# Reordering the beginning of a hybrid decoder layer: memory products first, then the products on a once-normed h

## The chip, the core and the metric

The kernel runs on one core of a Trainium2 chip. The metric is device microseconds of one execution. A profile of one execution shows, per engine, every instruction with its start and duration: TensorE (PE, with its weight loads as PEld), VectorE (DVE), ScalarE (ACT), GpSimd (POOL), and the queues that issue transfers (SP, and the transfer-issuing parts of ACT and POOL).

## The reference, cut to what matters

One layer, x of 512 x 2048 in f32, memory of 256 x 2048:

```
h = rmsnorm(x, norm_g)                      # one factor per token, times a gain per channel
(a_q, a_ckv, i_q, i_k, i_w, ..., mix_gate) = split(h @ w_in)
m_k, m_v = split(rmsnorm(mem, mem_norm_g) @ w_mem_kv)
ckv = rmsnorm(a_ckv, kv_norm_g);  a_k, a_v = split(ckv @ w_kv_up)
... three attention branches, gated, projected up, merged, then
x = x + merged @ w_o
```

All products are kept at nearly f32 accuracy: each factor is split into a high part (rounded to the chip's fast f32 form) and a low part (the rest), and three products high x high, high x low, low x high are summed.

## The kernel before

The activations stand transposed: h is 16 slices of 128 channels by 512 tokens, with high parts in `hth` and low parts in `htl`. Weights come from memory in units of 128 x 1024, three buffers deep (`wraw`); each half (512 columns) is split by `split`: ACT casts the high part `wh`, DVE subtracts to get the low part `wl`. A global counter of such halves is the program's clock: `next_hb()` advances it by one step, `step(i)` splits the half that is used four steps later (`LA = 4`) and then runs whatever `plan(i, f)` has put at this step. So all engines get their instructions in an order written out by hand, and each engine executes its own list strictly in order. Background generators (`pump`) advance by one `yield` a step and put their instructions between.

The program begins with these stages:

1. **g1** (16 steps): a group of 336 columns of w_in (the latent `a_ckv`, the index key and index weights) times h. Per step `x_split` makes a high and a low part of x times the gain, not yet of h; the token factor is applied to the result afterwards (L457, L459). ACT squares x (`x_sq`, L379) and POOL adds the squares into `accx` (L380). At the end `g_rms` turns the sum into the token factors `rx` and spreads them over a tile `rb`. A step has 12 products of 336 columns.
2. **mem** (32 steps): mem times w_mem_kv, 6 products of 512 columns a step, four PSUM banks. `m_split` splits two slices of mem every fourth step. Beside it `g_lat` norms the latent, and `g_comb` makes the final h: per round k (8 of them, over slices k and k+8) DVE norms x again with `rb` (L544), ACT casts high parts (L537), DVE and POOL make low parts (L534), and POOL forms four sums and differences of quarter blocks (L559 to L562), whose high parts ACT casts into `hx` (L572) and whose low parts POOL subtracts (L553). These sums feed a seven-product (Strassen-like) scheme that the rest of the kernel uses.
3. **kv** (3 units, n = 0, 1, 2): the latent times w_kv_up, 12 groups of 6 products of 512 columns; `kv_group` squares, sums (DVE `ss` L467), takes a power on POOL (`r`, L304), scales (`t`, L674) and transposes on PE (L678). Before n = 2 the program text waits until `g_comb` has put out all its instructions.
4. **pairs**: the large stage with seven products per weight pair, from the first `p<-hth,wh` on. Its first weights A11 and S1 are loaded by SP when the mem buffers are given back; POOL adds a further block onto S1 by a transfer that accumulates (L217) and sums S1 and A11 (`wS`, L211).

Of the kernel before, what the change touches and what calls it, by code (L numbers as in the profile page):

```python
# [110 lines left out]
def hybrid_layer(ctx: ExitStack, tc: tile.TileContext, xT, memT, memR, w_g1, w_un, w_up, params, consts, rel1, onehot, out):  # L111
# [286 lines left out]

    for c in range(8):
        if c:  # L400
            plan(2 * c - 8, lambda c=c: x_dma(c))
    for k in range(KT):
        plan(k - 4 - (k == 0), lambda k=k: x_split(k))
        plan(k - 3, lambda k=k: x_sq(k))
    i_mem = POS["mem", 0]
    for c in range(8):
        i = i_mem + 4 * c
# [12 lines left out]
    t = wp.tile([128, 1024], F32, tag="raw", bufs=3, name=nm("wraw"))  # L420
    for k in range(2):
        sync.dma_start(xf(k), xT[k].rearrange("p (a b) -> p a b", a=2))
        sync.dma_start(t[:, k * WG:k * WG + WG], w_g1[0, :, k * WG:k * WG + WG])
    tiles_["g1", 0] = t
    for i in range(-8, 0):
        step(i)
        if i == -6:
            sync.dma_start(cc, consts)

    def g_rms():  # L430

        sm = yield from take("sm")
        for i in range(4):
            mmf(sm[:, i:i + 1], accx[:, i * 128:i * 128 + 128], ones1)
        yield from lag("r0")
        done["rx"] = r = rsq(sm[:, :4], 4, 1.0 / D, EPS)
        give("sm")
        yield from lag("r1")
        b = yield from take("sm")
        bcast(b, r, 4)  # L440
        yield from lag("r2")
        act.copy(rb, b)
        give("sm")
        done["rb"] = True
# [81 lines left out]
    def g_comb():  # L526

        while "rb" not in done:
            yield

        nxt, f = {}, None

        def low(k, j, e):
            e.tensor_tensor(out=htl[:, k + 8 * j, :], in0=nxt[k][:, j, :], in1=hth[:, k + 8 * j, :].bitcast(F32), op=ALU.subtract)  # L534

        def high(k, j):
            act.copy(hth[:, k + 8 * j, :], nxt[k][:, j, :])  # L537

        def norm(k, j):
            if k < 8:  # L540
                if j == 0:
                    nxt[k] = cb.tile([128, 2, T], F32, tag="xr", bufs=2, name=nm("xr"))
                v = nxt[k][:, j, :].rearrange("p (a b) -> p a b", a=2)
                dve.scalar_tensor_tensor(v, xf(k + 8 * j), prm(P_NG + k + 8 * j), rb.rearrange("p (a b) -> p a b", a=2),  # L544
                                         op0=ALU.mult, op1=ALU.mult)

        norm(0, 0)
        norm(0, 1)
        yield
        for k in range(9):  # L550
            if k:
                low(k - 1, 0, dve)
                pool_e.tensor_tensor(out=hxt[k - 1][:, 3:6, :], in0=f, in1=hxt[k - 1][:, 0:3, :].bitcast(F32), op=ALU.subtract)  # L553
            if k == 8:
                break
            yield from lag("cb0")
            f = cb.tile([128, 3, 256], F32, tag="tf", bufs=1, name=nm("tf"))
            b11, b12, b21, b22 = (nxt[k][:, j, c:c + 256] for j in range(2) for c in (0, 256))
            pool_e.tensor_tensor(out=f[:, 1, :], in0=b12, in1=b22, op=ALU.subtract)  # L559
            pool_e.tensor_tensor(out=b12, in0=b11, in1=b12, op=ALU.subtract)  # L560
            pool_e.tensor_tensor(out=f[:, 0, :], in0=b22, in1=b12, op=ALU.add)
            pool_e.tensor_tensor(out=f[:, 2, :], in0=b21, in1=f[:, 0, :], op=ALU.subtract)  # L562
            high(k, 1)
            norm(k + 1, 0)
            yield from lag("cb1")
            low(k, 1, pool_e)
            yield from lag("cb2")
            high(k, 0)
            norm(k + 1, 1)
            yield from lag("cb3")  # L570
# [893 lines left out]
```

## Time and profile before

| | |
|---|---|
| three runs | 1613.4, 1618.41 (median), 1621.61 us |
| profiled execution | 1609.5 us, of which span 1607.7 us |
| PE busy in the span | 1506.1 us (94%) |
| DVE, ACT, POOL busy | 1281.3, 794.1, 665.8 us |
| granted TensorE clock, mean | 0.983 |

In the views a releaser ("<-") is what ended an engine's wait. Durations of consecutive instructions on one engine overlap a little, since the next starts before the last has quite ended. [...]

### The profile page before, as it was taken

To read this page: it belongs to the slowest core of one execution; us is meant where nothing else is said; L and a number is where in the kernel's file an instruction comes from. 1 tells how busy PE (TensorE), PEld (TensorE's weight loads), DVE (VectorE), ACT (ScalarE), POOL (GpSimd) and SP (SyncE) were. 2 spreads that over 40 slices of the span, in tenths; PEclk is the share of its full clock that TensorE was granted. 3 is DMA by queue.
4 is the path that set the end of the run, shared out by engine and by line. 5 is a ranking of instruction groups with operands and counts; after the bars stand their busy time and mean duration, and the time that the engine had idled before them with its cause. 6 is when DMAs were issued, how large, how long until landed. Compare 5 with 4: busy or idle time off the path is not lost.

```text
span 1607.7 us, 29512 instructions
## 1 busy us (share of the span) xinstructions
PE 1506.1 (94%) x11066; PEld 1418.6 (88%) x11066; DVE 1281.3 (80%) x1965; ACT 794.1 (49%) x1681; POOL 665.8 (41%) x548
## 2 busy tenths in 40 slices
PE   8778988989989999999999999999989999989999
PEld 6657988889889999999999899898989888869999
DVE  8997678999998678788777787887767567997786
ACT  7545466654545454555454545555545322434442
POOL 5675342333334344333333343333324013775453
PEclk9988999999999999999999999999999999989999
DMA  6337669445446655646555555455456655555774
GB/s 213 131 127 182 170 187 241 118 126 154 122 138 177 189 160 173 182 126 182 177 126 179 147 138 161 119 157 132 141 145 201 219 191 184 177 152 170 205 207 135
DMA packets 98792, 263.75 MB, mean 164 GB/s; under 512 B 10356, under 2 KB 24052, under 8 KB 98650
## 3 DMA queue, kind: packets, MB, share of 16 engines
q1 hardware_dynamic: 81050, 201.97, 35.9%
q0 software_dynamic: 15264, 55.58, 19.0%
q10 hardware_dynamic: 2336, 4.33, 1.1%
q8 instruction: 87, 1.43, 0.3%
q14 instruction: 55, 0.45, 0.1%
HBM read 237.12 MB, written 29.04 MB: 166 GB/s over the span
## 4 chain that ended last, share of the span: by engine, by line
PE 58%; DVE 23%; issue 7%; ACT 4%; DMA 3%; POOL 3%; SPq 0%; ACTq 0%; DVEq 0%; POOLq 0%
PE p L292 18%; PE p L293 18%; PE p L294 18%; DVE wl L276 12%; PE p L297 2%; ACT wh L274 2%; DVE Wk L850 1%; DMA wA<-in_w_un 1%; PE p L955 1%; DVE t L785 1%; DVE m L888 1%; POOL wS L211 1%; DVE Wk L889 1%; POOL r L304 1%; DVE htl L1266 1%
## 5 line engine op out<-in xcount | busy, mean ns | idle before, releaser
L292 PE MATMUL p<-hth,wh 128*128 128x256 f32 (+1 forms) x1792 | 529.7, 296 | 9.9 <-ACT hth L1264 5.5
L294 PE MATMUL p<-hth,wl 128*128 128x256 f32 (+1 forms) x1792 | 519.0, 290 | 1.5 <-DVE wl L276 1.4
L293 PE MATMUL p<-htl,wh 128*128 128x256 f32 (+1 forms) x1792 | 518.0, 289 | 2.3 <-DVE htl L1266 2.3
L276 DVE TENSOR_TENSOR wl<-wS,wh 128x512 fp32r<-128x512 f32 x318 | 318.3, 1013 | 98.7 <-ACT wh L274 94.6
L292 PE MATMUL p<-hx,wh 128*128 128x256 f32 x1272 | 370.4, 291 | 4.8 <-ACT kb L1084 3.3
L294 PE MATMUL p<-hx,wl 128*128 128x256 f32 x1272 | 363.1, 285 | 1.7 <-DVE wl L276 1.6
L276 DVE TENSOR_TENSOR wl<-wraw,wh 128x512 fp32r<-128x512 f32 (+2 forms) x346 | 302.5, 887 | 77.4 <-ACT wh L274 76.6
L292 PEld LDWEIGHTS p<-hth,wh 128*128 128x128 f32 x1792 | 343.8, 192 | 21.1 <-ACT hth L1264 5.7
L293 PE MATMUL p<-hx,wh 128*128 128x256 f32 x1272 | 361.9, 285 | 0.0
L293 PEld LDWEIGHTS p<-htl,wh 128*128 128x128 f32 x1792 | 343.7, 192 | 8.7 <-DVE htl L1266 2.6
L294 PEld LDWEIGHTS p<-hth,wl 128*128 128x128 f32 x1792 | 343.6, 192 | 6.8 <-DVE wl L276 3.0
L211 POOL TENSOR_TENSOR wS<-wS,wA 128x512 f32<-128x512 f32 x106 | 152.8, 1463 | 439.5 <-DMA wA<-in_w_un 247.4
L292 PEld LDWEIGHTS p<-hx,wh 128*128 128x128 f32 x1272 | 246.0, 193 | 10.4 <-ACT kb L1084 3.4
L274 ACT CAST wh<-wraw 128x512 fp32r<-128x512 f32 (+2 forms) x346 | 202.3, 590 | 105.4 <-PE p L293 66.6
L294 PEld LDWEIGHTS p<-hx,wl 128*128 128x128 f32 x1272 | 245.6, 193 | 3.4 <-DVE wl L276 3.4
L293 PEld LDWEIGHTS p<-hx,wh 128*128 128x128 f32 x1272 | 246.0, 193 | 1.1
L274 ACT CAST wh<-wS 128x512 fp32r<-128x512 f32 x318 | 193.8, 618 | 88.1 <-POOL wS L211 41.7
L276 DVE TENSOR_TENSOR wl<-wA,wh 128x512 fp32r<-128x512 f32 x212 | 171.9, 811 | 36.9 <-ACT wh L274 35.2
L211 POOL TENSOR_TENSOR wS<-wraw,wS 128x512 f32<-128x512 f32 x106 | 168.6, 1674 | 8.9 <-DVE wl L276 8.9
L274 ACT CAST wh<-wA 128x512 fp32r<-128x512 f32 x212 | 124.2, 618 | 72.1 <-DMA wA<-in_w_un 39.1
L304 POOL TENSOR_TENSOR r<-rv,cc 128x4 f32<-128x4 f32 (+2 forms) x30 | 41.6, 1388 | 136.9 <-DVE rv L303 136.9
L800 POOL TENSOR_TENSOR t<-u,u 128x256 f32<-128x256 f32 x35 | 37.4, 1068 | 124.2 <-DVE u L799 84.8
(225 smaller groups left out, 2108.4 us busy)
## 6 DMA issues: line engine op xcount, KB each, us to landing
wraw<-in_w_un SPq DMA_DIRECT2D x133, 512.0 KB, 5.4
wS<-in_w_un SPq DMA_DIRECT2D x53, 512.0 KB, 5.8
wA<-in_w_un SPq DMA_DIRECT2D x53, 512.0 KB, 3.7
wS<-in_w_un POOLq DMA_DIRECT2D x53, 512.0 KB, 7.7
wA<-in_w_un POOLq DMA_DIRECT2D x53, 512.0 KB, 5.2
th_d<-t SPq DMA_DIRECT2D x48, 256.0 KB, 4.4
t<-th_d SPq DMA_DIRECT2D x48, 256.0 KB, 3.0
wraw<-in_w_up SPq DMA_DIRECT2D x32, 384.0 KB, 3.7
```

The costliest lines, as they stand in the source:

```text
L211: pool_e.tensor_tensor(out=tiles_[key][:, s], in0=tiles_[a][:, s], in1=tiles_[b][:, s], op=op)
L274: act.copy(h[:, :w], s)
L276: e.tensor_tensor(out=l[:, :w], in0=s, in1=h[:, :w].bitcast(F32), op=ALU.subtract)
L292: pe.matmul(o, ah, bh, start=first, stop=False, skip_group_check=True)
L293: pe.matmul(o, ah, bl, start=False, stop=False, skip_group_check=True)
L294: pe.matmul(o, al, bh, start=False, stop=last, skip_group_check=True)
L297: pe.matmul(o, a, b, start=first, stop=last)
L304: pool_e.tensor_tensor(out=r[:, :n], in0=v[:, :n], in1=cc[:, C_NH:C_NH + n], op=ALU.pow)
L785: dve.tensor_tensor(out=t, in0=p, in1=ev[u], op=ALU.add)
L800: pool_e.tensor_tensor(out=o[1][:, 256:], in0=ev["u3"], in1=ev["u5"], op=ALU.subtract)
L850: dve.scalar_tensor_tensor(s, rl[:, :w], iwt[:, ti, h:h + 1], s, op0=ALU.mult, op1=ALU.add)
L888: dve.max(out=m8, in_=s)
```

## The change

The stages come in the order mem (11 of 16 slices, 22 steps), g1 (16 steps), mem (the last 10 steps), kv. While the first mem steps run, x is loaded by ACT's transfer queue, squared by ACT, and summed by DVE, one slice a step. Then the token factors are made (`rms_sum`, `rms_pow`, `rms_rows`, each planned at a step), and x is normed in place: `x_norm` writes h over x and casts the high part, `x_low` makes the low part. g1 thus uses the final h, in the order 0, 8, 1, 9, ..., and its result needs no factor. `g_comb` keeps only the quarter sums, all on DVE, with the high half-slices on ACT; POOL has no elementwise work left in the beginning except the powers. g1's weights are packed on the host in the new order of slices.

```diff
-    singles("g1", ...)
-    singles("mem", un[:16])
+    singles("mem", un[:K1])          # K1 = 11
+    singles("g1", [w_g1[k] for k in range(8)])
+    singles("mem2", un[K1:16])
...
-            sync.dma_start(xf(k), xT[k]...)                      # x_dma, two slices at a time
+            act.dma_start(xf(k), xT[k]...)
...
-        act.activation(hi, xf(k), AF.Copy, scale=prm(P_NG + k))  # x_split
-        dve.scalar_tensor_tensor(lo, xf(k), prm(P_NG + k), hi...)
-            pool_e.tensor_tensor(out=accx, in0=accx, in1=sq, op=ALU.add)
+        dve.tensor_tensor(out=accx, in0=accx, in1=sqs.pop(k), op=ALU.add)   # x_sum
+    def x_norm(k):
+        dve.scalar_tensor_tensor(xf(k), xf(k), prm(P_NG + k), rb..., op0=ALU.mult, op1=ALU.mult)
+        act.copy(hth[:, k, :]..., xf(k))
+    def x_low(k):
+        dve.tensor_tensor(out=lo, in0=xf(k), in1=hi.bitcast(F32), op=ALU.subtract)
...
+    KO = [k + 8 * j for k in range(8) for j in range(2)]
+    for k in range(KT):
+        plan(k - 6, x_dma(k)); plan(k - 2, x_sq(k)); plan(k - 1, x_sum(k))   # k > 0 for the sum
+    plan(KT, rms_sum); plan(KT + 1, rms_pow); plan(KT + 2, rms_rows)
+    for n, k in enumerate(KO):
+        plan(i_g1 - 2 + n, x_norm(k)); plan(i_g1 - 1 + n, x_low(k))
...
+    mem(range(K1))
     g1 = ...
-    act.activation(zt[:, i, :], g1[i][:, :WG], AF.Copy, scale=done["rx"][:, i:i + 1])
+    act.copy(zt[:, i, :], g1[i][:, :WG])
...
-    def g_comb():   # per k: norm twice, high twice, low on DVE and POOL, 5 POOL operations, lags cb0 to cb3
+    def g_comb():
+        def low(k):
+            dve.tensor_tensor(out=htl[:, k, 256:], in0=xf(k)[:, 1, :], in1=hth[:, k, 256:]..., op=ALU.subtract)
+            hx_new(k, F32R)
+            act.copy(hxt[k][:, 0:3, :], f)
+        def low3(k):
+            dve.tensor_tensor(out=hxt[k][:, 3:6, :], in0=f, in1=hxt[k][:, 0:3, :]..., op=ALU.subtract)
+        for k in range(8):
+            dve.tensor_tensor(out=f[:, 1, :], in0=b12, in1=b22, op=ALU.subtract)
+            dve.tensor_tensor(out=b12, in0=b11, in1=b12, op=ALU.subtract)
+            act.copy(hth[:, k, 256:], b12)
+            dve.tensor_tensor(out=f[:, 0, :], in0=b22, in1=b12, op=ALU.add)
+            dve.tensor_tensor(out=f[:, 2, :], in0=b21, in1=f[:, 0, :], op=ALU.subtract)
+            low(k)
+            yield from lag("cb0")
+            low3(k)
+            yield from lag("cb1")
-    mb = [...]; for k in range(KT): ...          # all 32 mem steps
+    mem(range(K1, KT))
...
+    while "lat" not in done:
+        pump()
```

The lags of `g_lat` (l0 to l3) go from 5, 3, 3, 4 to 2 each, and the fourth mem bank is `sm` instead of `o`. The tile of x for slices k and k+8 (`hx`) is the one that later holds round k's high and low parts of the quarter sums.

The first place is DVE's list during g1 (names: `hx` is x, `htl` low parts of h, `wl` low parts of weights, `t_2` the sum of squares). Before, one g1 step and the next:

```order
L372 SCALAR_TENSOR_TENSOR htl<-hx_149,pc,hth 128x512
L276 TENSOR_TENSOR wl_233<-wraw_162,wh_232 128x336
L372 SCALAR_TENSOR_TENSOR htl<-hx_164,pc,hth 128x512
L276 TENSOR_TENSOR wl_258<-wraw_162,wh_257 128x336
L372 SCALAR_TENSOR_TENSOR htl<-hx_166,pc,hth 128x512
```

In the changed kernel, at the same place in g1:

```order
L394 SCALAR_TENSOR_TENSOR hx_133<-hx_133,pc,rb_114 128x512
L278 TENSOR_TENSOR wl_560<-wraw_483,wh_559 128x336
L399 TENSOR_TENSOR htl<-hx_133,hth 128x512
L394 SCALAR_TENSOR_TENSOR hx_133<-hx_133,pc,rb_114 128x512
L278 TENSOR_TENSOR wl_579<-wraw_511,wh_578 128x336
L399 TENSOR_TENSOR htl<-hx_133,hth 128x512
```

A step has three instructions on DVE instead of two: the norm, which is now here and no longer in the mem stage, a weight split, and the low part, which needs ACT's cast of the normed slice in between.

The second place is one round of `g_comb`. Before, DVE's list in the mem stage (`xr` the normed x, `ml` low parts of mem); its quarter sums are on POOL:

```order
L276 TENSOR_TENSOR wl_859<-wraw_791,wh_858 128x512
L544 SCALAR_TENSOR_TENSOR xr_845<-hx_147,pc,rb_114 128x512
L276 TENSOR_TENSOR wl_875<-wraw_791,wh_874 128x512
L396 SCALAR_TENSOR_TENSOR ml_879<-mr_793,pc,mh_878 128x256 x2
L534 TENSOR_TENSOR htl<-xr_774,hth 128x512
L276 TENSOR_TENSOR wl_895<-wraw_827,wh_894 128x512
L544 SCALAR_TENSOR_TENSOR xr_912<-hx_149,pc,rb_114 128x512
L276 TENSOR_TENSOR wl_915<-wraw_827,wh_914 128x512
```

In the changed kernel, DVE's list for one round (`tf` the quarter sums):

```order
L562 TENSOR_TENSOR tf_954<-hx_141 128x256
L563 TENSOR_TENSOR hx_141<-hx_141 128x256
L565 TENSOR_TENSOR tf_954<-hx_141 128x256
L566 TENSOR_TENSOR tf_954<-hx_141,tf_954 128x256
L552 TENSOR_TENSOR htl<-hx_141,hth 128x256
L278 TENSOR_TENSOR wl_964<-wraw_889,wh_963 128x512
L557 TENSOR_TENSOR hx_961<-tf_954,hx_961 128x768
L278 TENSOR_TENSOR wl_977<-wraw_889,wh_976 128x512
```

and ACT's list for the same round of the changed kernel and the beginning of the next:

```order
L564 CAST hth<-hx_141 128x256
L554 CAST hx_961<-tf_954 128x768
L276 CAST wh_963<-wraw_889 128x512
L276 CAST wh_976<-wraw_889 128x512
L564 CAST hth<-hx_149 128x256
```

DVE now does five short operations and one long one a round where it did two norms and a low part, and POOL none where it did six. ACT's 768-column cast stands ahead of the weight casts, and it writes over the tile of x that DVE's L552 reads.

The third place is POOL's list at the end of `g_comb`. Before:

```order
L562 TENSOR_TENSOR tf_1095<-xr_1044,tf_1095 128x256
L534 TENSOR_TENSOR htl<-xr_1044,hth 128x512
L553 TENSOR_TENSOR hx_1153<-tf_1095,hx_1153 128x768
L217 DMA wS_227_1124<-in_w_un 128x1024
L211 TENSOR_TENSOR wS_245_1188<-wS_227_1124,wA_228_1126 128x512
L304 TENSOR_TENSOR r_1205<-rv_1204,cc 128x2
```

In the changed kernel, from the first power of the program:

```order
L306 TENSOR_TENSOR r_464<-rv_463,cc 128x4
L306 TENSOR_TENSOR r_912<-rv_911,cc 128x4
L218 DMA wS_216_1083<-in_w_un 128x1024
L212 TENSOR_TENSOR wS_237_1162<-wS_216_1083,wA_217_1085 128x512
L306 TENSOR_TENSOR r_1180<-rv_1179,cc 128x2
```

The transfer onto S1 no longer stands behind 48 elementwise operations of `g_comb`; the powers of the kv groups still stand behind the sum `wS`.

## Rows read from the trace of the kernel before

**Rows 1.** stretches: window, busy (xcount) of PE, PEld, DVE, ACT, POOL, clock, DMA, GB/s

```profile
0.00:45.50 45.50, 38.64 (x211) 32.64 (x212) 37.57 (x43) 29.96 (x58) 23.77 (x20) 1.00 0.66 219
45.50:129.00 83.50, 65.63 (x237) 48.85 (x236) 82.33 (x85) 46.44 (x86) 63.03 (x50) 0.86 0.39 135
129.00:149.60 20.60, 13.64 (x54) 10.47 (x53) 10.54 (x26) 7.33 (x19) 9.75 (x11) 0.83 0.66 154
149.60:1607.70 1458.10, 1388.23 (x10571) 1326.63 (x10569) 1150.87 (x1813) 710.34 (x1522) 569.25 (x468) 0.99 0.57 164
```

**Rows 2.** DVE, timeline in g1: start us, us, line, operation

```profile
28.14 0.74 DVE L372 SCALAR_TENSOR_TENSOR htl<-hx,pc,hth 128x512 fp32r<-128x512 f32 x1
28.80 0.49 DVE L276 TENSOR_TENSOR wl<-wraw,wh 128x336 fp32r<-128x336 f32 x1
29.22 1.78 DVE L372 SCALAR_TENSOR_TENSOR htl<-hx,pc,hth 128x512 fp32r<-128x512 f32 x1
```

**Rows 3.** POOL, timeline of the same stretch

```profile
28.93 3.23 POOL L380 TENSOR_TENSOR t<-t,sq 128x512 f32<-128x512 f32 x2 [2.16 <-ACT sq L379]
```

**Rows 4.** DVE, timeline of one round in the mem stage

```profile
107.03 2.88 DVE L276 TENSOR_TENSOR wl<-wraw,wh 128x512 fp32r<-128x512 f32 x2
...
110.50 0.68 DVE L276 TENSOR_TENSOR wl<-wraw,wh 128x512 fp32r<-128x512 f32 x1
...
116.86 2.89 DVE L276 TENSOR_TENSOR wl<-wraw,wh 128x512 fp32r<-128x512 f32 x2
```

**Rows 5.** PE, timeline in the mem stage

```profile
61.03 0.39 PE L294 MATMUL mb<-wh,ml 128*128 128x512 f32 x1
61.26 0.39 PE L292 MATMUL mb<-wh,mh 128*128 128x512 f32 x1
...
79.73 0.79 PE L293 MATMUL mb<-wl,mh 128*128 128x512 f32 x1 [2.25 <-DVE wl L276]
```

**Rows 6.** POOL and DVE, timeline of the tail of kv

```profile
130.82 0.40 DVE L467 TENSOR_REDUCE ss<-sq 128x2 f32<-128x256 f32 x1
...
136.55 1.25 POOL L211 TENSOR_TENSOR wS<-wS,wA 128x512 f32<-128x512 f32 x1 [7.00 <-DMA wS<-in_w_un]
137.77 1.38 POOL L304 TENSOR_TENSOR r<-rv,cc 128x2 f32<-128x2 f32 x2
138.51 0.42 DVE L674 TENSOR_TENSOR t<-pk,r 128x256 f32<-128x256 f32 x1 [6.16 <-POOL r L304]
```

**Rows 7.** PE, timeline, first product of the pairs

```profile
149.67 0.36 PE L292 MATMUL p<-hth,wh 128*128 128x256 f32 x1
```

**Rows 8.** ACT and PE, timeline of the first products

```profile
5.09 0.45 ACT L274 CAST wh<-wraw 128x336 fp32r<-128x336 f32 x1
...
5.59 0.42 PE L292 MATMUL g<-wh,hth 128*128 128x336 f32 x1
```

**Rows 9.** windows at the start, columns as in Rows 1

```profile
5.00:10.00 5.00, 4.30 (x21) 2.92 (x20) 2.94 (x5) 3.38 (x8) 0.13 (x1) 1.00 1.02 351
10.00:20.00 10.00, 7.43 (x45) 6.59 (x44) 9.57 (x7) 10.00 (x21) 9.32 (x7) 1.00 0.57 206
```

**Rows 10.** a group of DVE over the whole span

```profile
L1284 DVE TENSOR_TENSOR f<-m,f 128x256 f32<-128x256 f32 x1 | 0.4, 418 | 0.0
```

**Rows 11.** groups of 0 to 150 us: count, busy us, mean ns

```profile
L274 ACT CAST wh<-wraw 128x512 fp32r<-128x512 f32 x38 | 23.0, 617 | 7.5 <-DMA wraw<-in_w_un 4.1 <-PE g L294 3.4
...
L572 ACT CAST hx<-tf 128x768 fp32r<-128x768 f32 x8 | 6.6, 830 | 0.9 <-POOL tf L562 0.7
```

**Rows 12.** ACT and its transfer queue, timeline

```profile
247.16 0.63 ACTq L722 DMA_DIRECT2D ra_d<-rel_d  x1
247.68 0.61 ACT L833 CAST stk<-t 64x512 fp32r<-64x512 f32 x1
```

**Rows 13.** transfer issues of the page: KB, median us to landing

```profile
wS<-in_w_un SPq DMA_DIRECT2D x53, 512.0 KB, 5.8
...
wS<-in_w_un POOLq DMA_DIRECT2D x53, 512.0 KB, 7.7
```

More of the change, by code (lines that the diff above doesn't have):

```diff
@@ L91 @@
          ("S3", "T3", False), ("S4", "B22", False), ("A22", "T4", True)]
+K1 = 11
 LA = 4
@@ L397, in m_split @@
         MS[c] = (h, l)
-    for c in range(8):
[L400 to L407, printed above, removed]
+    KO = [k + 8 * j for k in range(8) for j in range(2)]
+    for k in range(KT):
+        plan(k - 6, lambda k=k: x_dma(k))
+        plan(k - 2, lambda k=k: x_sq(k))
+        if k:
+            plan(k - 1, lambda k=k: x_sum(k))
+    plan(KT, rms_sum)
+    plan(KT + 1, rms_pow)
+    plan(KT + 2, rms_rows)
+    i_g1 = POS["g1", 0]
+    for n, k in enumerate(KO):
+        plan(i_g1 - 2 + n, lambda k=k: x_norm(k))
+        plan(i_g1 - 1 + n, lambda k=k: x_low(k))
+    for c in range(8):
+        i = POS["mem", 2 * c] if 2 * c < K1 else POS["mem2", 2 * c - K1]
         plan(i - 8, lambda c=c: m_dma(c))
@@ L419, in hybrid_layer, with mem @@
     sync.dma_start(pc, params)
[L420 to L424, printed above, removed]
+    for f in at.pop(-8):
+        f()
+    raw(("mem", 0), un[0])()
     for i in range(-8, 0):
         step(i)
[L427 to L444, printed above, removed]
+    plan(2, lambda: sync.dma_start(cc, consts))
+    mb = [psum(t, "mb") for t in ("qk", "qk", "pt", "sm")]
+    def mem(ks):
+        for k in ks:
+            mh, ml = MS[k // 2]
+            for half in range(2):
+                wh, wl = next_hb()
+                for i in range(2):
+                    s = slice(i * 128, i * 128 + 128)
+                    mm3(mb[2 * half + i], mh[:, k % 2, s], ml[:, k % 2, s], wh, wl, k == 0, k == KT - 1)
+                pump()
+    mem(range(K1))
     g1 = [psum(t, "g1") for t in ("o", "a", "b", "c")]
-    for k in range(KT):
+    for n, k in enumerate(KO):
         wh, wl = next_hb()
@@ L456, in hybrid_layer @@
         if i % 2 == 0:
-            act.activation(zt[:, i, :], g1[i][:, :WG], AF.Copy, scale=done["rx"][:, i:i + 1])
+            act.copy(zt[:, i, :], g1[i][:, :WG])
         else:
-            dve.tensor_scalar(out=zt[:, i, :], in0=g1[i][:, :WG], scalar1=done["rx"][:, i:i + 1], scalar2=None, op0=ALU.mult)
+            dve.tensor_copy(out=zt[:, i, :], in_=g1[i][:, :WG])
     dve.tensor_scalar(out=hb, in0=prm(P_GB, 48), scalar1=0.5, scalar2=None, op0=ALU.mult)
@@ L493, in g_lat @@
             dve.scalar_tensor_tensor(ckl[:, j, :], b[j], prm(P_KVG + j), ckh[:, j, :].bitcast(F32), op0=ALU.mult, op1=ALU.subtract)
+        done["lat"] = True
     def g_ik():
@@ L526, in g_comb @@
     def g_comb():
[L528 to L570, printed above, removed]
+        f = None
@@ L571, in g_comb @@
+        def low(k):
+            dve.tensor_tensor(out=htl[:, k, 256:], in0=xf(k)[:, 1, :], in1=hth[:, k, 256:].bitcast(F32), op=ALU.subtract)
             hx_new(k, F32R)
             act.copy(hxt[k][:, 0:3, :], f)
+        def low3(k):
+            dve.tensor_tensor(out=hxt[k][:, 3:6, :], in0=f, in1=hxt[k][:, 0:3, :].bitcast(F32), op=ALU.subtract)
+        for k in range(8):
+            f = cb.tile([128, 3, 256], F32, tag="tf", bufs=2, name=nm("tf"))
+            b11, b12, b21, b22 = (xf(k + 8 * j)[:, c, :] for j in range(2) for c in range(2))
+            dve.tensor_tensor(out=f[:, 1, :], in0=b12, in1=b22, op=ALU.subtract)
[7 more added lines that the diff above has]
+            yield from lag("cb1")
@@ L576, in hybrid_layer @@
     pump.back(g_comb())
-    mb = [psum(t, "mb") for t in ("qk", "qk", "pt", "o")]
-    for k in range(KT):
-        if k % 2 == 0:
-            mh, ml = MS.pop(k // 2)
-        for half in range(2):
-            wh, wl = next_hb()
-            for i in range(2):
-                s = slice(i * 128, i * 128 + 128)
-                mm3(mb[2 * half + i], mh[:, k % 2, s], ml[:, k % 2, s], wh, wl, k == 0, k == KT - 1)
-            pump()
+    mem(range(K1, KT))
     def scaled(r, n):
@@ L599, in hybrid_layer @@
     give("pt")
+    give("sm")
     mp_s.close()
```

41 lines of the change are left out of this document (24 added, 17 removed).

## The prediction

> **What bounds the kernel now.** I read the page's 40 slices first: PE is busy above 80% everywhere except in the first tenth. So I cut the span there [rows 1]. After 149.6 us PE is busy 1388 of 1458 us; the change touches only what is before, 150 us in which PE is busy 118. In the long second stretch (45.5 to 129 us, the mem stage) the busy engine is DVE, 82.3 of 83.5 us, at a mean clock of 0.86.
>
> Second, DVE's timeline, to see why it is full. The same instruction takes 0.74 us at 28.14 and 1.78 at 29.22 [rows 2], and the second lies inside a POOL addition that runs from 28.93 on [rows 3]: while POOL works on tiles, DVE's two-input operations take about twice as long. In the mem stage a round of four steps takes 9.83 us, from 107.03 to 116.86 [rows 4], with weight splits of 0.68 when POOL is idle and 1.44 (2.88 for two) when it isn't. PE's products follow each other at 0.23 us at full clock [rows 5], so four steps of six are 5.5 us. DVE sets the round; PE waits, 2.25 us at one place [rows 5].
>
> Third, the tail of kv. DVE has its sum ready at 130.82, but the power on POOL comes only at 137.77, since POOL stands at the sum `wS`, which waits 7.00 us for a transfer; DVE waits 6.16 us for the power and PE for DVE [rows 6]. The first pair product starts at 149.67 [rows 7]. That is the moment I compute for the changed kernel; what follows is the same work, bound by PE.
>
> **The change, stage by stage.** Durations are those with POOL idle, since POOL now has only powers. Back to back an instruction costs 0.07 less than its duration (28.14 + 0.74 against 28.80 [rows 2]); from one engine to the next I add 0.05 (5.09 + 0.45 to 5.59 [rows 8]).
>
> Stage 1, 22 mem steps. The first product now needs a weight unit of 0.52 MB instead of 0.17, and x shares the engines; 0.35 to 0.85 MB more at 351 GB/s [rows 9] is 1.0 to 2.4 us, and a second weight cast and two casts of mem stand before it on ACT, about 1.2: 5.6 + 1.7 + 1.2 = 8.4 us. PE needs 22 x 6 x 0.23 = 30.4. While x comes (14 steps), two steps move 1.18 MB (a weight unit, two slices of x, half a tile of mem), 3.36 us at 351 GB/s against 2.74 of PE: 7 x 0.6 = 4.3 more. End: 43 us. DVE lies below it: 22 splits of 0.61 and 4 of 0.42, 15 sums of 0.61, 12 splits of mem of 0.41 (a two-input operation on 256 columns [rows 10]) are 29 us; ACT has 26 casts of weights, 16 squares and 12 small casts, about 31 us by 0.62 for 512 columns [rows 11]. ACT's issuing of x costs it nothing: an issue of 0.63 us ran beside casts [rows 12]. If the transfers run faster, the floor is PE's, 39; bounds 39 to 47 while the rate stays above 300 GB/s.
>
> Stage 2, g1. A step is a chain: norm 0.74 (as L372 with POOL idle [rows 2]), ACT's cast 0.62, low part 0.61, three handovers: 2.07 us; the weight split of 0.42 lies beside the cast. PE's 12 products of 336 columns are 12 x 0.15 = 1.83, so the chain sets the pace. The first norm can start about three mem steps before stage 1 ends, its low part is there 2.5 us before, 15 more chains are 31.0, and the last step's products take 1.9: 30.5 us after stage 1, at 73.5. Bounds 29.3 (PE alone) to 35 (no overlap).
>
> Stage 3, the quarter sums with the last 10 mem steps and kv 0 and 1. Per round DVE does four operations of 256 columns, 0.42 each [rows 10], each waiting for the one before (1.8 with handovers), and the low part, 0.42. Then ACT's 768-column cast, 0.83 [rows 11], may start, for it writes over the tile that the low part reads; behind it on ACT stands the weight cast, 0.62, which DVE's next instruction needs: 1.55 us in which DVE waits. Then split 0.61, the long low part (0.88 back to back: an estimate, 0.68 for 512 columns plus 256 x 1.05 ns, the slope from 0.49 for 336 to 0.68 for 512 [rows 2, 4]), split 0.61. Sum 5.9. Five rounds are 29.3; the three beside kv, with two copies out of PSUM and fewer splits, 6.9 + 4.0 + 5.9 = 16.8; the start 1.0; the latent's sums, product and low parts and one split of mem, 4.7. Together 51.8 us: DVE reaches the sum of rows 6 at 125.3 instead of 130.82. Bounds: 41, if DVE needn't wait for those two casts, to 57, if handovers cost twice as much. PE's two steps are 2.7 us in a round of 5.9, and at half clock, which it may get after such gaps (0.86 on average in the second stretch of rows 1, with gaps of 2.25 us), still below the round: the clock costs nothing here.
>
> [...]
>
> Stage 4, the tail. The transfer onto S1 stood behind POOL's 48 quarter operations; now it needs only S1, which SP loads when the last mem product is done: three rounds and two steps of PE into stage 3, some 24 us. With 5.8 us for the load and 7.7 for the transfer onto it [rows 13] it is there some 14 us before the powers want POOL. From the start of the sum to `t` I count 0.40 + 0.17 + 0.70 + handovers = 1.4 instead of 138.51 - 130.82 = 7.7. So `t` comes at 126.7, 11.8 us earlier. From there to the first pair product it is 11.2 us as before: the same list, on a PE that has idled before it too.
>
> Sum: 43 + 30.5 + 51.8 + 1.4 + 11.2 = 137.9 against 149.7, a gain of 11.8. The profiled execution's 1609.5 us becomes 1597.7. The median of the runs shown, 1618.41, lies 0.55% above that execution; I scale: 1606.5 us.
>
> **Rivals.**
> The transfers are slow (the slower side). Stage 1 moves 11.8 MB (11 weight units 5.8, x 4.2, mem 1.6, small ones 0.3). At the 206 GB/s of the next window [rows 9] it would end at 57 + 3 = 60 us instead of 43, and the kernel at 1615 in the profile's time, 1624 in the median's. It decides below 11.8 MB / 51.8 us = 228 GB/s. Against it: in that window the share was 0.57, so the engines weren't full, while 351 came with a share of 1.02. For it: those 351 held for five microseconds and from one issuing engine. [...] Chance 0.08.
>
> DVE doesn't wait for the casts in stage 3, because rounds overlap better than I drew: seven rounds lose 1.55 us each, 10.9 us more gain: 1586.8, median 1595.5. For it: before, ACT waited only 0.9 us in all before its eight 768-column casts [rows 11]. Against: the order of ACT's list and the tile written over. Chance 0.14.
>
> The wait at `wS` stays as long, since it is the transfers that are late and not POOL: then only stages 1 to 3 count, 5.5 us: 1604, median 1613, within 0.5%. For it: 7.00 us of that wait are put down to the transfer. Chance 0.10.
>
> The change does what it says, but the pairs don't start sooner, or give it back, because their weights come no earlier: no gain, 1618. Against: PE's 95% after 149.6. Chance 0.06.
>
> **How the numbers follow.** My forecast has 0.62; its own range from the stages' bounds is 1600 to 1614. The range over the cases, leaving the slow transfers out: 1594 to 1617. About 0.5%, 8.1 us, is what a measurement of this kernel can tell from no change. Nine tenths of my forecast lie beyond it, with the second rival: 0.56 + 0.14 = 0.70 faster. Within: 0.05 + 0.10 + 0.06 = 0.21. Slower: 0.08, and 0.01 of the forecast's upper end: 0.09.
>
> **What would show it.** First pair product near 138 us. Stage 1: first mem product near 8.4, the 22nd step done near 43, transfers above 300 GB/s over it, PE at full clock; much later with DMA share near 1 is the first rival. Stage 2: norms about 2.07 us apart. Stage 3: DVE's weight splits at 0.68 throughout (if they stay above 1 us, POOL wasn't the cause), and in each round a wait of about 1.5 us of DVE for `wh`; none is the second rival. Stage 4: POOL waits for the DVE sum and not for a transfer; if DVE still waits over 5 us for the power, it is the third. I am wrong if the stretch after the first pair product gets longer by more than 3 us, or if the first pair product isn't at least 8 us earlier.

## The result, and the profile after

The changed kernel takes 1627.0 us (median of 7 runs, 1622.9 to 1631.4), the kernel before 1619.9 beside it (7 runs, 1611.3 to 1621.8): 1.0057 of before, 95% interval 1.0031 to 1.0084. It is slower by half a per cent; 1606.5 was forecast. The first product of the pairs comes at 157.33 us instead of 149.67 [rows 7]: 7.7 us later; the medians differ by 7.1. The loss lies where the change is.

The profile after, cut at the first product of each stage (the forecast's four stages), columns as in [rows 1]:

```profile
0.00:48.40 48.40, 41.05 (x155) 30.43 (x155) 32.10 (x59) 30.65 (x58) 1.42 (x5) 0.93 0.75 273
48.40:93.56 45.16, 33.64 (x194) 29.46 (x192) 28.81 (x49) 17.39 (x35) 0.00 (x0) 1.00 0.28 90
93.56:144.58 51.02, 32.23 (x118) 24.77 (x116) 39.48 (x80) 24.32 (x46) 3.44 (x3) 0.83 0.36 103
144.58:157.33 12.75, 9.37 (x36) 7.30 (x37) 9.74 (x23) 6.28 (x15) 7.98 (x9) 0.73 0.61 143
157.33:1625.00 1467.67, 1398.92 (x10571) 1338.47 (x10569) 1143.80 (x1813) 710.24 (x1522) 571.62 (x468) 0.98 0.57 163
```

| stage | forecast, us | measured | difference |
|---|---|---|---|
| 1, 22 mem steps | 43 | 48.4 | +5.4 |
| 2, 16 g1 steps | 30.5 | 45.2 | +14.7 |
| 3, mem, quarter sums, kv | 51.8 | 51.0 | -0.8 |
| 4, tail | 12.6 | 12.75 | +0.1 |
| first pair product | 137.9 | 157.3 | +19.4 |

In stage 2 no engine is full: PE is busy 33.6 of 45.2 us, DVE 28.8, ACT 17.4. That is the mark of a chain that runs from engine to engine. DVE's timeline of one step there (start, duration, line, operation; in brackets its wait and whom it waited for):

```profile
59.62 0.74 DVE L394 SCALAR_TENSOR_TENSOR hx<-hx,pc,rb 128x512 f32<-128x512 f32 x1
61.42 0.51 DVE L278 TENSOR_TENSOR wl<-wraw,wh 128x336 fp32r<-128x336 f32 x1 [1.06 <-ACT wh L276]
61.85 0.69 DVE L399 TENSOR_TENSOR htl<-hx,hth 128x512 fp32r<-128x512 f32 x1
62.45 0.74 DVE L394 SCALAR_TENSOR_TENSOR hx<-hx,pc,rb 128x512 f32<-128x512 f32 x1
```

and ACT's, of the same step:

```profile
60.40 0.62 ACT L395 CAST hth<-hx 128x512 fp32r<-128x512 f32 x1 [1.84 <-DVE hx L394]
60.92 0.47 ACT L276 CAST wh<-wraw 128x336 fp32r<-128x336 f32 x1
```

Read the starts as one chain: norm 59.62, cast of the slice 60.40, cast of the weights 60.92, their split 61.42, low part 61.85, next norm 62.45. The gaps are 0.78 + 0.52 + 0.50 + 0.43 + 0.60 = 2.83 us. DVE stands 1.06 us before the split, although the low part behind it could start at about 61.05, 0.65 us after the start of the slice's cast (as it does in e8 below). The cast that the split wants is for a step four later; it stands behind the slice's cast on ACT. So a prefetch that nobody needs yet sits in the middle of the chain.

The table of waits, 48.40 to 93.56 us (total, times, longest):

```profile
DVE wl L278 <- ACT wh L276: 16.3, 15, 1.2
ACT hth L395 <- DVE hx L394: 28.0, 15, 2.0
```

DVE loses 16.3 us of stage 2 to this one kind of wait, and another 9.7 of stage 3. There it is the wait that the forecast drew, 1.42 us a round beside 1.55; a round takes 5.62 (109.13 to 114.75) beside 5.9:

```profile
109.13 0.42 DVE L562 TENSOR_TENSOR tf<-hx 128x256 f32<-128x256 f32 x1
...
110.84 0.42 DVE L552 TENSOR_TENSOR htl<-hx,hth 128x256 fp32r<-128x256 f32 x1
112.67 0.69 DVE L278 TENSOR_TENSOR wl<-wraw,wh 128x512 fp32r<-128x512 f32 x1 [1.42 <-ACT wh L276]
113.28 0.95 DVE L557 TENSOR_TENSOR hx<-tf,hx 128x768 fp32r<-128x768 f32 x1
114.15 0.69 DVE L278 TENSOR_TENSOR wl<-wraw,wh 128x512 fp32r<-128x512 f32 x1
114.75 0.42 DVE L562 TENSOR_TENSOR tf<-hx 128x256 f32<-128x256 f32 x1
```

Stage 1's loss is at its end. PE's timeline (an x8 row is eight small products in one row):

```profile
35.10 1.51 PE L299 MATMUL p<-cc,t 128*128 128x1 f32 x8 [2.90 <-DVE t L377]
36.47 0.77 PE L294 MATMUL mb<-wh,mh 128*128 128x512 f32 x1
...
38.32 0.63 PE L295 MATMUL mb<-wl,mh 128*128 128x512 f32 x1
38.75 0.63 PE L296 MATMUL mb<-wh,ml 128*128 128x512 f32 x1
...
41.73 1.35 PE L299 MATMUL p<-cc,r 128*128 128x128 f32 x8
42.84 0.48 PE L294 MATMUL mb<-wh,mh 128*128 128x512 f32 x1
43.16 0.39 PE L295 MATMUL mb<-wl,mh 128*128 128x512 f32 x1
```

and the windows around it:

```profile
24.00:32.00 8.00, 7.38 (x32) 5.48 (x30) 7.42 (x13) 6.82 (x13) 0.00 (x0) 1.00 1.04 393
32.00:36.00 4.00, 1.10 (x7) 0.90 (x7) 3.96 (x8) 3.87 (x9) 0.00 (x0) 0.94 0.60 197
36.00:43.00 7.00, 7.00 (x24) 5.84 (x25) 2.22 (x6) 0.64 (x2) 1.21 (x1) 0.55 0.35 98
```

PE waits 2.90 us for the last sum of squares; in the 4 us around this wait it is busy 1.10. Behind it the granted clock is 0.55 on average from 36 to 43, and 0.50 in each microsecond from 36 to 42: the products follow each other at 0.43 us instead of 0.23 [rows 5]. Before the wait the 16 steps were done at 32.2, earlier than the 34.8 that the forecast's terms give (8.4 + 16 x 1.38 + 4.3), since the transfers ran at 393 GB/s. Then come 2.9 of wait, 2.5 for the small products, which the forecast didn't count (1.37 + 1.11), and 2.5 for twelve products at the low clock (5.26 against 2.76): with the 2.6 won before, they make up the 5.4 to within 0.1.

The last of these terms isn't fixed. The kernels e2 and e3 below have the same instructions here; PE waits for the same sum 2.17 us in e2 and 2.04 in e3, and from 36 to 43 their windows show

```profile
36.00:43.00 7.00, 7.00 (x39) 6.05 (x39) 3.90 (x10) 2.66 (x6) 1.21 (x1) 1.00 0.38 100
36.00:43.00 7.00, 7.00 (x25) 5.80 (x25) 2.05 (x6) 0.70 (x3) 1.21 (x1) 0.56 0.35 98
```

The clock stays up in e2, and its stage 1 ends at 45.8; it falls in e3, which ends at 48.2. The changed kernel's own second profile (a2) lies between, 0.77 and 46.9. So up to 2.6 us at the first pair product can come from stage 1 without any edit to it.

The tail went as forecast. POOL, and DVE's sum and `t`, against [rows 6]:

```profile
121.99 1.07 POOL L218 DMA_DIRECT2D wS<-in_w_un  x1 [19.13 <-DVE ckl L513]
127.78 1.25 POOL L212 TENSOR_TENSOR wS<-wS,wA 128x512 f32<-128x512 f32 x1 [4.72 <-DMA wS<-in_w_un]
145.27 1.38 POOL L306 TENSOR_TENSOR r<-rv,cc 128x2 f32<-128x2 f32 x2 [16.23 <-DVE rv L305]
```

```profile
144.58 0.41 DVE L487 TENSOR_REDUCE ss<-sq 128x2 f32<-128x256 f32 x1
...
146.02 0.42 DVE L664 TENSOR_TENSOR t<-pk,r 128x256 f32<-128x256 f32 x1 [0.30 <-POOL r L306]
```

The sum onto `wS` is over 16 us before the power is wanted; from the sum to `t` it is 1.44 us instead of 7.7.

### The profile page after: what moved, and what is told of

Read it like the earlier page. It is cut to its first block, busy times and chain, and to the rows that moved or that the text cites. A ratio compares the mean times of both kernels' runs of the same rounds, so it can differ in the third digit from the quotient of the medians.

```text
span 1625.0 us, 29434 instructions
## 1 busy us (share of the span) xinstructions
PE 1515.2 (93%) x11066; PEld 1430.4 (88%) x11066; DVE 1253.9 (77%) x2020; ACT 788.9 (49%) x1673; POOL 584.5 (36%) x485
## 4 chain that ended last, share of the span: by engine, by line
PE 62%; DVE 22%; issue 5%; ACT 4%; DMA 4%; POOL 2%; SPq 0%; ACTq 0%; DVEq 0%; POOLq 0%
PE p L294 19%; PE p L296 19%; PE p L295 19%; DVE wl L278 11%; PE p L299 3%; ACT wh L276 2%; DMA wraw<-in_w_un 1%; DVE Wk L842 1%; PE p L947 1%; DVE m L880 1%; DVE t L777 1%; DMA og<-og_d 1%; DMA og_d<-t 1%; DVE Wk L881 1%; DVE hx L394 1%
## 5 line engine op out<-in xcount | busy, mean ns | idle before, releaser
L278 DVE TENSOR_TENSOR wl<-wraw,wh 128x512 fp32r<-128x512 f32 (+2 forms) x346 | 269.3, 790 | 113.0 <-ACT wh L276 111.1
L294 PEld LDWEIGHTS p<-hx,wh 128*128 128x128 f32 x1272 | 249.0, 196 | 10.9 <-ACT kb L1076 3.8
L296 PEld LDWEIGHTS p<-hx,wl 128*128 128x128 f32 x1272 | 249.1, 196 | 3.5 <-DVE wl L278 3.5
L295 PEld LDWEIGHTS p<-hx,wh 128*128 128x128 f32 x1272 | 249.5, 196 | 1.1
L1219 ACT ACTIVATE t<-t,hb 128x512 f32<-128x512 f32 x48 | 34.7, 724 | 107.7 <-DVE t L777 103.4
```

What stands on the lines that cost most here:

```text
L278: e.tensor_tensor(out=l[:, :w], in0=s, in1=h[:, :w].bitcast(F32), op=ALU.subtract)
L294: pe.matmul(o, ah, bh, start=first, stop=False, skip_group_check=True)
L295: pe.matmul(o, ah, bl, start=False, stop=False, skip_group_check=True)
L296: pe.matmul(o, al, bh, start=False, stop=last, skip_group_check=True)
L1219: act.activation(z, z, AF.Tanh, bias=hb[:, 16 * j + d + x:16 * j + d + x + 1], scale=0.5)
```

## The experiments

The theory: the changed kernel loses in stage 2, because the weights' cast and split are put out between the slice's cast and its low part. Rivals: the step is set by transfers, or by engines that slow each other; or the pairs give the time back. Where each kernel stands, from its profile (us from the start; ratios against the kernel before, with intervals where several runs were timed). Stage 1 ends with the first product of g1, and g1 with the first product behind it:

| kernel | order | end of stage 1 | end of g1 | first pair product | ratio |
|---|---|---|---|---|---|
| before | g1, mem | - | 45.9 | 149.7 | 1 |
| after | mem, g1, mem | 48.4 | 93.6 | 157.3 | 1.0057 [1.0031, 1.0084] |
| e1 | as after | 46.8 | 76.3 | 139.8 | 0.9922 [0.9892, 0.9951] |
| e9 | as after | 48.5 | 84.6 | 149.0 | one run |
| e8 | as after | 47.2 | 89.7 | 154.4 | one run |
| e2 | as after | 45.8 | 90.9 | 149.5 | 0.999 [0.9975, 1.0004] |
| e3 | as after | 48.2 | 77.7 | 136.1 | 0.9858 [0.9839, 0.9876] |
| e4 | as after | 46.8 (24 steps) | 76.2 | 131.8 | 0.9864 [0.9839, 0.989] |
| e5 | as after | 51.0 | 96.1 | 161.0 | 1.0067 [1.0042, 1.0093] |
| e6 | as after | 49.0 | 94.1 | 157.8 | one run |
| e7a | as before | - | 38.2 | 142.3 | one run |
| e7 | as before | - | 38.1 | 129.9 | 0.9854 [0.9831, 0.9877] |

**e1: the slice's cast behind the weights' cast.**

```diff
-        act.copy(hth[:, k, :]..., xf(k))                 # in x_norm
+    def x_high(k):
+        act.copy(hth[:, k, :]..., xf(k))
...
-        plan(i_g1 - 2 + n, lambda k=k: x_norm(k))
+        plan(i_g1 - 3 + n, lambda k=k: x_norm(k))
+        plan(i_g1 - 2 + n, lambda k=k: x_high(k))
```

> Only the order of the 16 steps on h's first products is changed: the cast of a normed slice is put out one step later, behind that step's weight cast, and the slices are normed one step earlier. Theory A (VectorE's split of the weights waits for a cast that stands behind the slice's cast on ScalarE, and the slice's low part stands behind that split): without it VectorE's own list is the longest, 0.75 + 0.68 + 0.42 to 0.51 = 1.85 to 1.94 us a step, the stage takes about 31 us instead of 46, the first product of the pairs comes at about 142 us instead of 157.3, and the time is about 0.995 of the kernel before. Rival B (the step of 2.83 us is set by the weights' transfers, or by VectorE and ScalarE being slower beside each other): the step stays above 2.6 us, the first pair product at 153 or later, the time at 1.003 to 1.006. Rival C (what is won here is lost among the pairs): first pair product at 142, but the time still 1.005 of before.

g1 takes 29.4 us, the first pair product comes at 139.8, the ratio is 0.9922: theory A. DVE's timeline of a step of e1:

```profile
50.96 0.75 DVE L394 SCALAR_TENSOR_TENSOR hx<-hx,pc,rb 128x512 f32<-128x512 f32 x1
51.62 0.50 DVE L278 TENSOR_TENSOR wl<-wraw,wh 128x336 fp32r<-128x336 f32 x1
52.04 0.69 DVE L401 TENSOR_TENSOR htl<-hx,hth 128x512 fp32r<-128x512 f32 x1
52.64 0.75 DVE L394 SCALAR_TENSOR_TENSOR hx<-hx,pc,rb 128x512 f32<-128x512 f32 x1
```

The same instructions with the same durations, no wait in brackets, 1.68 us from norm to norm. PE is now what limits: it is busy in all of the 29.45 us, 16 times its 1.84:

```profile
46.84:76.29 29.45, 29.45 (x194) 29.45 (x193) 27.01 (x47) 17.45 (x33) 0.00 (x0) 1.00 0.46 143
```

Three lines moved in the list bring the first pair product 17.5 us forward, 15.7 of them in g1; 1.6 lie in stage 1, as much as a2 shows without an edit.

**e9: norm before low part.** The low part is taken out of the chain, the split stays in it.

```diff
-        plan(i_g1 - 1 + n, lambda k=k: x_low(k))
+        if n:
+            plan(i_g1 - 2 + n, lambda k=KO[n - 1]: x_low(k))     # now behind the norm of that step
...
```

> The changed kernel, but in each of the 16 steps on h VectorE norms the next slice before it takes the low part of the last one; ScalarE's order stays as changed. The chain of a step as the corrected theory has it: norm 0.75, the slice's cast 0.62, the weights' cast 0.47 behind it, their split 0.50, four handovers of 0.02 to 0.08: 2.35 to 2.5 us, the low part now lying beside the casts; the stage 38 to 40 us instead of 45.2, first pair product at 150 to 152. Rival (the step is no such chain, and e1 won by its earlier norm alone): 2.8 us and 157.

DVE's timeline of e9:

```profile
60.72 0.51 DVE L278 TENSOR_TENSOR wl<-wraw,wh 128x336 fp32r<-128x336 f32 x1 [0.46 <-ACT wh L276]
61.15 0.74 DVE L394 SCALAR_TENSOR_TENSOR hx<-hx,pc,rb 128x512 f32<-128x512 f32 x1
61.81 0.68 DVE L399 TENSOR_TENSOR htl<-hx,hth 128x512 fp32r<-128x512 f32 x1
62.95 0.51 DVE L278 TENSOR_TENSOR wl<-wraw,wh 128x336 fp32r<-128x336 f32 x1 [0.46 <-ACT wh L276]
```

The step is 2.23 us, which is 2.83 less the low part's 0.60. g1 takes 36.1 us and the first pair product comes at 149.0, so the rival (2.8 us and 157) is refuted. My expectation of 2.35 to 2.5 was too long, because I added durations: recorded ones overlap what follows by 0.07 to 0.1. Added from starts, 0.78 + 0.52 + 0.50 + 0.43 make the 2.23.

**e8: the split out of the chain, on GpSimd.**

```diff
-    POOL_LO = ()
+    POOL_LO = range(22, 38)
```

> The changed kernel, but the split of the weights (the subtraction that makes wl) of the 16 steps on h stands on GpSimd: nothing is reordered, only the one term that the prediction laid beside the cast is taken out of VectorE's list. Theory A: the chain of a step is then norm 0.75, cast 0.62, low part 0.68 and three handovers, 2.1 us where GpSimd does not slow VectorE, and up to 2.6 where it does as in the kernel before (mean 1.16 to 1.23 us for the operations that take 0.68 to 0.74 alone); stage 34 to 42 us instead of 45.2, first pair product at 146 to 154. Rival B (the step's length is not made by the split's place): 2.8 us or more, first pair product at 157 or later.

The step is 2.69 us and the stage 42.5, both a little beyond theory A's long end (2.6 and 42) and short of the rival's 2.8. The timelines of DVE, ACT and POOL in e8:

```profile
60.99 0.69 DVE L399 TENSOR_TENSOR htl<-hx,hth 128x512 fp32r<-128x512 f32 x1 [0.69 <-ACT hth L395]
61.60 1.40 DVE L394 SCALAR_TENSOR_TENSOR hx<-hx,pc,rb 128x512 f32<-128x512 f32 x1
63.69 0.69 DVE L399 TENSOR_TENSOR htl<-hx,hth 128x512 fp32r<-128x512 f32 x1 [0.69 <-ACT hth L395]
```

```profile
63.04 0.62 ACT L395 CAST hth<-hx 128x512 fp32r<-128x512 f32 x1 [1.70 <-DVE hx L394]
```

```profile
61.42 1.04 POOL L278 TENSOR_TENSOR wl<-wraw,wh 128x336 fp32r<-128x336 f32 x1 [1.66 <-ACT wh L276]
```

The chain is now the one of the forecast: norm, cast, low part. But the norm takes 1.40 instead of 0.74, since GpSimd's split starts 0.18 before it; 2.69 - 0.66 = 2.03 would be the forecast's step; no run shows it without this slowing. The norm ends 0.54 us after GpSimd's operation ends at 62.46: of the 0.86 us in which the two lie beside each other, the norm, which started later, loses 0.66. What the two contend for, no run shows. So moving the split gains 0.14 us a step, and ordering it (e1) about 1.0.

**e2: the rounds of the quarter sums.** The low part and the cast of three quarters come one step later, the low part of three a round later.

```diff
-            low(k)                  # htl, then the 768-column cast
             yield from lag("cb0")
-            low3(k)
+            low(k)
+            if k:
+                low3(k - 1, prev)
+            high3(k, f)             # the 768-column cast
+            prev = f
...
```

> Only the rounds that combine the quarters are changed: low part of one quarter and cast of three come one step later, the low part of three one round later, so that no weight cast stands behind the 768-column cast that VectorE waits for. Theory A: VectorE's wait of 1.42 us in each round goes, a round is its own work (2 x 0.69 + 5 x 0.42 + 0.95 = 4.4 us against 5.62), stage 3 takes about 43 us instead of 51.3, the first pair product comes at about 149, the time is about 1.000 of before. Rival B (the rounds are set by TensorE or by the transfers, and the wait is slack): round stays at 5.5 or more, first pair product 156 to 158, time 1.005.

Stage 3 takes 43.9 us up to the sum (90.9 to 134.85) instead of 51.0, and the ratio is 0.999: theory A, though a round is 4.98 and not 4.4 (105.63 to 110.61 in its trace), since the 768-column cast still stands ahead of the next weight cast and 0.60 of the 1.42 us remains:

```profile
109.54 0.69 DVE L278 TENSOR_TENSOR wl<-wraw,wh 128x512 fp32r<-128x512 f32 x1 [0.60 <-ACT wh L276]
```

That the first pair product, at 149.5, meets the expected 149 is in part luck: the tail behind the sum is 1.9 us longer than after's 12.75, and stage 1 ended 2.6 us earlier without an edit there. Of the 7.8 us gained up to that point, the edit gave 5.2.

**e3: both orders.** The two edits together.

> Both reorderings together. Theory A: the gains add, 15.5 + 8.5 = 24 us: first pair product at about 133, time about 0.990 of the kernel before. Rival B (the second stage won only moves the wait to the transfer of the pairs' first tiles or to GpSimd's sum of them, which were late in the kernel before): first pair product not before 140, time 0.995. Rival C (lost among the pairs): 133, and a time above 0.996.

First pair product at 136.1, 21.2 us earlier than after, not 24: stage 3 keeps its 7 us, the tail behind the sum is 1.6 longer than after's 12.75. The time, 0.9858, is better than that point promises (13.6 us, 0.992). Its profile shows 1461.0 us behind the point; that is inside the 1458.0 to 1467.7 of the two unedited kernels' profiles (b2 and a2 below), so it shows no gain among the pairs, and what makes the time better stays open.

**e4: the sums' end two steps later**, on top of e3.

```diff
-K1 = 11
+K1 = 12
-    plan(KT, rms_sum); plan(KT + 1, rms_pow); plan(KT + 2, rms_rows)
+    plan(KT + 2, rms_sum); plan(KT + 3, rms_pow); plan(KT + 4, rms_rows)
```

> Both reorderings as in e3, and the 4 products that end the sums of squares stand two steps later on TensorE (K1 = 12, so that two steps of the memory's products move from the third stage to the first). Theory A (TensorE's wait of 2.9 us for VectorE's last sum, and the granted clock of 0.55 to 0.76 that the trace shows behind it, cost the first stage 4.3 us against the forecast): the wait and the low clock go, the stage with 24 steps ends near 47 as it did with 22, the third has two steps less, and the first pair product comes at 132 to 133 instead of 136.1; time about 0.983 of before. Rival B (TensorE would wait as long for the memory's weights, whose transfers fill the stage): a wait of 2 to 3 us at another place, first pair product at 135 to 137, time 0.986.

The wait before the products of the sums is gone, and so is the low clock that e3 has there. The windows of e4 there:

```profile
36.00:43.00 7.00, 6.63 (x38) 5.42 (x37) 4.15 (x10) 3.35 (x8) 1.04 (x1) 1.00 0.56 149
43.00:46.80 3.80, 3.80 (x19) 3.12 (x18) 3.72 (x7) 2.70 (x6) 0.00 (x0) 1.00 0.41 114
```

38 instructions of PE in seven microseconds instead of 24. 24 steps end at 46.8, where 22 ended at 48.4, and the first pair product is at 131.8: theory A there. The time, 0.9864, can't be told from e3's: 4.4 us are 0.27%, less than either interval is wide.

**e7 and e7a: the sums without the new order.** In the kernel before, `pool_e` becomes `dve` in the sums of squares alone (e7a), and also in the quarter sums and two low parts (e7).

```diff
-            pool_e.tensor_tensor(out=accx, in0=accx, in1=sq, op=ALU.add)
+            dve.tensor_tensor(out=accx, in0=accx, in1=sq, op=ALU.add)      # e7a and e7
-            pool_e.tensor_tensor(out=f[:, 1, :], in0=b12, in1=b22, op=ALU.subtract)
+            dve.tensor_tensor(out=f[:, 1, :], in0=b12, in1=b22, op=ALU.subtract)      # e7, and five more
```

> The kernel before in its own order, with only its elementwise sums before the pairs (squares of x, quarter sums, two low parts) moved from GpSimd to VectorE: the one part of the change without the other. Theory A (the two engines slowed each other; alone VectorE's operations take 0.42 to 0.75): the 16 steps on x take about 37 us instead of 45.5, a round over the memory's weights about 9.1 instead of 9.83 (VectorE then has 2 x 0.75 + 2 x 0.68 + 4 x 0.68 + 4 x 0.42 + 0.95 + 0.84 in it), and the first pair product comes at 129 to 135 instead of 149.7; time 0.987 to 0.992 of before: the new order alone would be what costs. Rival B (the sums only change engines; VectorE has no room): first pair product at 148 to 153, time 1.000 to 1.003, and the order is what has to be mended.

> The kernel before with only the 15 sums of x's squares on VectorE; quarter sums and low parts stay on GpSimd. This splits the 19.8 us that all sums on VectorE won. Expected: the first stage as with all of them (its last product at 37 instead of 45), the rounds over the memory's weights as in the kernel before (9.8 us), first pair product at 141 to 143. If the rounds are shorter too, the two engines' share of them was not what made them long.

Both go the way of theory A: in e7a g1 ends 7.7 us earlier, the first pair product comes 7.3 earlier, and the rounds stay at 9.81; with all sums a round is 8.3 (9.1 was expected), the first pair product 19.8 us earlier, and the time a little below the expected 0.987 to 0.992. The windows of e7 up to it:

```profile
0.00:38.12 38.12, 36.62 (x214) 33.26 (x215) 31.49 (x58) 30.07 (x59) 1.63 (x5) 1.00 0.79 265
38.12:123.40 85.28, 66.94 (x270) 50.76 (x269) 79.14 (x150) 50.90 (x99) 8.67 (x9) 0.94 0.52 159
```

DVE has more instructions here than before (216 against 152 up to the first pair product), and yet it is busy 114.4 us there instead of 130.5: a weight split of 512 columns takes 0.68 us on average where it took 1.12. PE is 36.6 of 38.1 us busy in g1 and DVE 79.1 of 85.3 behind it. With 0.9854 this is as fast as e3 and e4: once its lists are mended, the new order shows no advantage over the old one.

**e5: sums of squares back on GpSimd** in the changed kernel (`dve` becomes `pool_e` in `x_sum`).

> The changed kernel with the 15 sums of x's squares back on GpSimd, all else as changed: what the sums on VectorE are worth in the first stage. Theory A (the two engines slow each other, and the stage is VectorE's as much as the transfers'): VectorE loses 0.68 of its 1.65 us a step but its splits take 1.1 instead of 0.68, GpSimd's sum takes 2 to 3 us a step, the sums end some 10 us later, and the first pair product comes at 162 to 168; time 1.003 to 1.007 of the changed kernel, 1.008 to 1.012 of before. Rival B (the transfers alone set the stage, at 390 GB/s): first pair product 156 to 158, time as the changed kernel's.

In e5 DVE's splits and POOL's sums lie beside each other:

```profile
24.69 5.17 DVE L278 TENSOR_TENSOR wl<-wraw,wh 128x512 fp32r<-128x512 f32 x3
```

```profile
26.23 3.08 POOL L377 TENSOR_TENSOR t<-t,sq 128x512 f32<-128x512 f32 x2 [0.31 <-ACT sq L374]
```

1.72 us a split instead of 0.69. The first pair product is 3.6 us later than after's, 5.5 later than in its second profile (5 to 11 were expected, since I put GpSimd's sum at 2 to 3 us and it takes 1.5). The time can't be told from after's. So by the first pair product this part of the change was worth having, a little less in the new order than in the old (7.3); the time doesn't show it.

**e6: x's transfers issued by SyncE** (`act.dma_start` becomes `sync.dma_start` in `x_dma`).

> The changed kernel with x's 16 transfers issued by SyncE beside the weights' instead of by ScalarE: does the second issuing engine bring the 390 to 398 GB/s of the first stage? Theory A (it doesn't; the 16 DMA engines are full at a share of 1.03 to 1.05, and the 351 GB/s before were five microseconds with small pieces among them): 385 to 398 GB/s again from 16 to 32 us, end of the first stage and first pair product within 2 us of the changed kernel's 48.4 and 157.3. Rival B (one issuing engine reaches 351 GB/s): the stage's 11.8 MB take 3.4 us longer, end of the first stage at 50 to 53, first pair product at 159 to 162.

Theory A. The windows of e6, to be laid beside after's 393 GB/s:

```profile
16.00:24.00 8.00, 7.76 (x34) 6.00 (x33) 7.26 (x13) 6.58 (x13) 0.00 (x0) 1.00 1.05 390
24.00:32.00 8.00, 7.16 (x30) 5.13 (x29) 7.88 (x14) 7.08 (x15) 0.00 (x0) 1.00 1.04 394
```

One issuing engine fills the transfers as two do: with x issued by SyncE they move 390 and 394 GB/s in these two windows, in after, with x issued by ScalarE, 394 and 393, at the same shares of 1.05 and 1.04.

**b2 and a2: both kernels a second time.**

> The kernel before, unchanged, profiled a second time: how far the first pair product and the span behind it move from run to run. Expected: first pair product within 0.5 of 149.7, and 1462 to 1470 us behind it instead of 1458, since its profiled span of 1607.7 lies below the median of its runs (1618 to 1622); then the 9.7 us that the changed kernel's profile shows more behind that point are the runs' own spread. Rival (the change does slow the pairs): 1458 again.

> The changed kernel, unchanged, profiled a second time beside it: first pair product at 157 to 158; behind it 1461 to 1468 us if the spread is the runs' own, 1467 to 1468 if the change made the pairs slower.

Before: first pair product at 148.9, 1463.8 us behind it; after: 155.4, and 1463.0. So no loss among the pairs shows, and the 1458.0 and 1467.7 of the first profiles were spread. Stage 2 takes 45.2 us in a2 too; the 1.9 us by which its first pair product comes earlier are mostly stage 1's (46.9 instead of 48.4). The difference at the first pair product is 6.5 us here, 7.7 in the first profiles.

## Why the prediction was wrong

- **Stage 2, the step that failed.** "The weight split of 0.42 lies beside the cast": it doesn't, it lies in the chain. The term of 2.07 us a step was 2.83, and 3.16 in the last two, where the prefetched weights have 512 columns: from the first norm (45.45) to the last (88.61) it is 43.2 us instead of 15 x 2.07 = 31.1, which is 12.1 of the 14.7. Of the others 1.6 are the first norm, which starts 2.95 us before the stage where the forecast's 2.5 + 2.07 put it 4.6 before, and 1.0 the last chain with its products (4.95 instead of 4.0). The forecast's price of a chain of three fits e8 less its contention, 2.03 (its three handovers of 0.05 would make 2.12, two make the 2.07), and e1 and e9 show that order alone makes the rest. With this stage at its forecast the first pair product would have come at 142.6, ahead of 149.7. The evidence was in the lists ahead of the prediction: DVE's has `wl` between norm and low part. I hadn't laid ACT's list of g1 beside it, where `wh` stands behind the slice's cast. In stage 3 I did exactly this, and came within 0.8 us.
- **Stage 1** was mis-sized by 5.4 us: 2.5 for small products left out, 2.9 of wait for a sum that I had on time, 2.5 for the clock behind that wait, a term that e2's profile doesn't have. With 48.4 it lies beyond the bounds of 39 to 47; a2 and e2 end inside them. I had added up DVE's work (29 us) and seen that it fits, which says nothing on when its last piece is done. Its first 16 steps were 2.6 us faster than forecast.
- **Stages 3 and 4** were right, in the mechanism and in the size: splits at 0.69 with POOL idle, 1.42 of wait a round, no wait at `wS` by the time the power is wanted. (The slope behind the long low part is 1.08 ns a column and not 1.05; it took 0.95 us, as forecast.)
- **The rivals.** Slow transfers: refuted, 393 GB/s from 24 to 32 us. No wait for the casts in stage 3: refuted by the trace; e2 shows that it could be had in part. The wait at `wS` stays: refuted. Given back among the pairs: the stretch behind the first pair product was 9.6 us longer in the first profiles, which by the forecast's own sign (3 us) would have meant it; b2 and a2, 1463.8 and 1463.0, don't bear it out. The kernel became slower by a way that was none of these; the upper bound of stage 2 (35) allowed for missing overlap, not for a longer chain.
- What stays open: the timed gains of e1, e2, e3, e4 and e7 are 1.4 to 9.5 us larger than their first pair products say. For e1, e2 and e4 that lies inside the intervals; for e3 (by 6 us) and barely for e7 it doesn't, and no run here tells why.

## What to carry to other kernels

When a step passes a slice from engine to engine and back, lay the lists of all the engines in it side by side and follow the starts: whatever stands between two links on any list is a link too, a prefetch with its own wait above all. Busy sums say that a stage fits, not when its last piece is done. When a change has two parts, price and try each alone: here the moved sums alone were worth 1.5%, and the rest of the change lost 2.0% until two of its lists were mended.

## What the runs showed of the hardware

A norm on VectorE went from 0.74 to 1.40 us by a single GpSimd split of 1.04 that started 0.18 earlier (e8), so here even short work on GpSimd that came first cost VectorE 0.66 us. And a wait of 2.9 us on TensorE, in a stretch of four microseconds with 1.1 of work, was followed by some six at a granted clock of 0.50: 2.5 us on twelve products, nearly as much as the wait itself. That didn't always follow: after 2.17 us of the same wait the clock stayed at 1.00 (e2), after 2.04 it fell to 0.56 on average from 36 to 43 (e3), and no run here tells what decides. Where the wait was gone (e4), it stayed at 1.00.
